# One encoder layer on one core: a second group of tile pairs by seven products in the last projection, with part of its weights prepared in the mixer

## The chip, the cores and the metric

The kernel runs on one core of one Trainium2 chip. The time is the device time of one execution, in microseconds (us), the median of several runs; one more execution was recorded by the hardware profiler, and every view below is of that one. Times inside a view count from the start of its span. The engines are TensorE (PE; PEld is its weight load), VectorE (DVE), ScalarE (ACT), GpSimd (POOL) and SyncE (SP, which here issues nearly all transfers).

## The reference

One layer of an encoder, on 512 tokens of width 1024, all in float32, with weights drawn at random:

```python
f = swiglu(rms_norm(h, ffn1_pre_g), ffn1_w1, ffn1_w3, ffn1_w2)   # (silu(x @ w1) * (x @ w3)) @ w2, D_FF = 2816
h = h + 0.5 * rms_norm(f, ffn1_post_g)
u = rms_norm(h, mix_pre_g)                                       # the mixer
q, k, v, xr, xg = split(u @ w_in)
y_a = (rg_lru(causal_conv(xr)) * gelu(xg)) @ w_lru_out
y_b = swa_sink_attention(q, k, v, sinks, bias) @ w_attn_out
g = sigmoid(u @ w_gate + b_gate)
h = h + rms_norm((g[0] * y_a + g[1] * y_b) @ w_o, mix_post_g)
f = swiglu(rms_norm(h, ffn2_pre_g), ffn2_w1, ffn2_w3, ffn2_w2)
h = h + 0.5 * rms_norm(f, ffn2_post_g)
```

The change is about the last matrix product of the second feed-forward part, `silu(...)*(...) @ ffn2_w2`: a hidden array of 2816 x 512 (features by tokens) against weights of 2816 x 1024, called w2b in the kernel. The first feed-forward part's is w2a.

## The kernel before

**Precision.** Each float32 operand is split into a high part (ScalarE copies it into the format that TensorE multiplies) and a low part (VectorE subtracts the high part from the operand). Each product is three matmuls: high by high, high by low, low by high.

**Stages.** w1a/w3a and w2a (first feed-forward part); the mixer, in the order xr, wg 0 to 7, wk, wv, wq, xg, then attention woven with lru, wq and wg 8 to 15, then wao and wo; w1b/w3b and w2b (second part). The 2816 features are 22 tiles of 128 rows. Most of w1/w3 is done by `Pairs`, which multiplies pairs of feature tiles by seven products of quarter blocks in place of eight (Winograd's form of Strassen's algorithm), on sums of blocks.

**w2_gemm.** The output (512 tokens by 1024) stands in all eight banks of PSUM as four token tiles by two halves. `W2[nm]` gives: how many tiles are multiplied plainly at first (24 matmuls of 512 columns a tile), how many pairs of tiles form the group that is multiplied by seven products, how many plain tiles come last (RF, four in w2b), and the planner's fill. In w2b it is 10 plain tiles, one group of 4 pairs, 4 last tiles. For a pair the hidden side is four quarters c (`h_plain`) and four sums of them s (`h_sums`), the weight side the blocks b11, b21 (`w_b1`), b22 and the sums t1, t2 (`w_t12`), t3 (`w_t34`) and t4 (`w_t4`), each with a high and a low part. `prod` runs one product over all pairs of the group (12 matmuls for each of two token tiles); between products banks are copied aside (`out_copy`, ScalarE, into tiles "kp") and added (`add_in`, VectorE). A group has a fixed cost of such copies and additions.

**Order of the work.** The program is laid out by hand. `point()` is called after every 12 matmuls or so; work is put on a list with `later(n, fn, rank)` and issued n points on. In `w2_gemm` a small planner gives each preparing step a due time (`PT` 5.44 a plain tile, `PB` 1.36 a product and pair) and a cost, goes through them backwards with `W2_LEAD` 2.5 us to spare and a fill of 0.95, and so finds the point at which each is issued. `task` issues a step's high part at once and its low part with the next step (`flush`).

**Memory.** All large tiles come from one pool of `NSLOT` = 43 slots of 4 KB a partition. An instruction whose result has no free slot waits until a slot's last reader is done. `uT` (32 KB a partition, outside the pool) holds the input of w1b/w3b and is lent to `w2_gemm` in eight regions of 4 KB. Transfers are issued by SP in program order (`dma_one`, `dma_to`), each also when its slot is free; a weight tile is 512 KB.

Of the kernel before, what the change touches and what calls it, by code (L numbers as in the profile page):

```python
# [51 lines left out]
def hybrid_layer(ctx: ExitStack, tc: tile.TileContext, a: dict, out: bass.AP):  # L52
# [42 lines left out]
    apart = {}  # L95

# [8 lines left out]
    def want_w2(name):  # L105

        first, n = W2[name][:2]
        apart.update((len(order) + first + i, i % 2) for i in range(2 * n))
        want(name, FT)
# [20 lines left out]

    loaded = set()
# [282 lines left out]

    def w2_gemm(nm, hid, gpost_name, scale, gpre_name, first, h_src, h_dst):

        W2_A, W2_S, RF, W2_FILL = W2[nm]
# [3 lines left out]
        pairs_ = list(range(W2_A, W2_A + 2 * W2_S, 2))  # L421

        def regions():
            for j in range(4):
                for e in range(2):
                    yield uT[:, e, 2 * j : 2 * j + 2, :].rearrange("p a b -> p (a b)")

        free_uT = list(regions())

        def room(name):  # L430
            return free_uT.pop(0) if free_uT else slot([P, D], F32R, name=name)

        def h_plain(f):
            H[f] = {"c": (room("ch"), room("cl"))}
            return H[f]["c"], hid.c[f].rearrange("p a b -> p (a b)")

        def h_sums(f):
            c = hid.c.pop(f)
            if any(x[0] is H[f]["c"][0] for x in pend):
                flush()  # L440
            a11, a12, a21, a22 = c[:, 0, :256], c[:, 1, :256], c[:, 0, 256:], c[:, 1, 256:]
            dve.tensor_tensor(out=a22, in0=a21, in1=a22, op=ALU.add)
            dve.tensor_tensor(out=a21, in0=a11, in1=a21, op=ALU.subtract)
            dve.tensor_tensor(out=a11, in0=a22, in1=a11, op=ALU.subtract)
            dve.tensor_tensor(out=a12, in0=a12, in1=a11, op=ALU.subtract)
            H[f]["s"] = (room("sh"), room("sl"))
            return H[f]["s"], c.rearrange("p a b -> p (a b)")

        def raw(f):
            if f not in W:  # L450
                k = base + f
                dma_to(k + 2)
                W[f] = {"r": (raws.pop(k), raws.pop(k + 1))}
            return W[f]["r"]

        def whole(f, a, b, src):
            hi, lo = slot([P, D], F32R, name="bh"), slot([P, D], F32R, name="bl")
            W[f][a] = (hi[:, :QH], lo[:, :QH])
            W[f][b] = (hi[:, QH:], lo[:, QH:])
            return (hi, lo), src  # L460

        def w_b1(f):
            return whole(f, "b11", "b21", raw(f)[0])

        def w_t12(f):
            r1, r2 = raw(f)
            s = slot([P, D], name="T12")
            dve.tensor_tensor(out=s[:, :QH], in0=r2[:, :QH], in1=r1[:, :QH], op=ALU.subtract)
            dve.tensor_tensor(out=s[:, QH:], in0=r2[:, QH:], in1=s[:, :QH], op=ALU.subtract)
            return whole(f, "t1", "t2", s)  # L470

        def w_t34(f):
            r1, r2 = raw(f)
            dve.tensor_tensor(out=r2[:, :QH], in0=r2[:, QH:], in1=r2[:, :QH], op=ALU.subtract)
            dve.tensor_tensor(out=r1[:, QH:], in0=r1[:, QH:], in1=r1[:, :QH], op=ALU.subtract)
            dve.tensor_tensor(out=r1[:, QH:], in0=r1[:, QH:], in1=r2[:, :QH], op=ALU.subtract)
            return whole(f, "t3", "b22", r2)

        def w_t4(f):
            r1 = W[f].pop("r")[0]  # L480
            t = slot([P, 2, QH], F32R, name="t4")
            W[f]["t4"] = (t[:, 0, :], t[:, 1, :])
            return W[f]["t4"], r1[:, QH:]

# [11 lines left out]
        def task(fn, f):  # L496
            one = fn(f)
            if one is not None:
                one = hi_part(*one)
            flush()  # L500
            if one is not None:
                pend.append(one)

        def tile_(k):
            dma_to(base + k + 1)
            hT = slot([P, 2, SEQ], F32R, name="hT")
            one = hi_part((hT[:, 0, :], hT[:, 1, :]), hid.f[k])
            hid.f[k] = None
            hid.t[k] = hT
            p = slot([P, D], F32R, name="whi"), slot([P, D], F32R, name="wlo")  # L510
            two = hi_part(p, raws.pop(base + k))
            pairs[base + k] = p
            st["split"] = base + k + 1
            flush()
            pend.extend((one, two))

        n0, F = W2_A + 2 * W2_S, FT - RF
        PT, PB = 5.44, 1.36 * W2_S
        ta = PT * W2_A
        tb = ta + 7 * PB  # L520
        tf = tb + PT * (F - n0)
        plan = [(PT * k, 1.75, tile_, k) for k in range(2, W2_A)]
        for i, f in enumerate(pairs_):
            d = 0.68 * i
            plan += [(ta + d, 1.14, h_plain, f), (ta + d, 1.14, w_b1, f), (ta + 2 * PB + d, 2.5, h_sums, f), (ta + 2 * PB + d, 2.4, w_t12, f)]
            plan += [(ta + 4 * PB + d, 3.0, w_t34, f), (ta + 6 * PB + d, 0.6, w_t4, f)]
        plan += [(tb + PT * (k - n0), 1.75, tile_, k) for k in range(n0, F)]
        plan += [(tf + 0.68 * (k - F), 1.75, tile_, k) for k in range(F, FT)]
        plan += [(ta + PB * (p + 0.5 * i + 0.5) + 1.5, 0.61, None, 0) for p in range(1, 7) for i in range(2)]
        plan.sort(key=lambda x: x[0])  # L530
        times = [PT / 2 * i for i in range(1, 2 * W2_A + 1)]
        times += [ta + PB / 2 * i for i in range(1, 15)]
        times += [tb + PT / 2 * i for i in range(1, 2 * (F - n0) + 1)]
# [17 lines left out]
        for k in range(2):  # L551
            w[k] = take(k)
        for tt in ((0, 1), (2, 3)):
            for t in tt:
                if t not in acc:
                    acc[t] = [bank("acc"), bank("acc")]
            for k in range(2):
                for t in tt:
                    mm_tok(acc[t], hid[k], t, w[k], k == 0, False)
                    if t % 2:  # L560
                        point()
# [11 lines left out]
        def add_in(b, name, i):  # L573
            dve.tensor_tensor(out=b, in0=b, in1=keep[name][:, i, :], op=ALU.add)

        for k in range(2, W2_A):
            w[k] = take(k)
            for t in range(NT):
                mm_tok(acc[t], hid[k], t, w[k], False, k == W2_A - 1)
                if k == W2_A - 1:  # L580
                    if t:
                        out_copy("z" if t < 2 else "y", t % 2, acc[t][1])
                    if t == 1:
                        out_copy("z", 0, acc[0][1])
                if t % 2:
                    point()
# [3 lines left out]
        st["get"] += 2 * W2_S  # L590
        def prod(b, i, ak, bk, start):
            for n_, f in enumerate(pairs_):
                wh, wl = W[f][bk]
                kind, blk = ak
                h, l = H[f][kind]
                c = slice(blk * 256 + i * P, blk * 256 + i * P + P)
                s_ = start and n_ == 0
                pe.matmul(b, h[:, c], wh, start=s_, stop=False, skip_group_check=True)  # L598
                pe.matmul(b, h[:, c], wl, start=False, stop=False, skip_group_check=True)  # L599
                pe.matmul(b, l[:, c], wh, start=False, stop=n_ == W2_S - 1, skip_group_check=True)  # L600

        def drop(*ks):
            for f in pairs_:
                for k_ in ks:
                    W[f].pop(k_)

        def fin(n, fn):
            later(n, fn, 0)

        for i in range(2):  # L610
            prod(Y[i], i, ("c", 0), "b11", True)
            out_copy("a", i, Y[i])
            point()
        for i in range(2):
            prod(X[i], i, ("c", 2), "b21", False)
            fin(1, lambda i=i: add_in(X[i], "a", i))
            point()
        for i in range(2):
            prod(Z[i], i, ("s", 3), "t1", True)
            dve.tensor_tensor(out=keep["y"][:, i, :], in0=Z[i], in1=keep["y"][:, i, :], op=ALU.add)  # L620
            point()
        drop("b11", "b21")
        for i in range(2):
            prod(Y[i], i, ("s", 0), "t2", False)
            dve.tensor_tensor(out=keep["z"][:, i, :], in0=Y[i], in1=keep["z"][:, i, :], op=ALU.add)
            point()
# [862 lines left out]
```

## Time and profile before

| | |
|---|---|
| median of 3 runs | 1131.6 us (1131.3 to 1131.66) |
| the profiled execution | 1131.66 us; its span 1129.9 us |
| granted TensorE clock | 0.998 of full |
| PE / DVE / ACT busy in the span | 1118.5 / 867.6 / 604.9 us |
| DMA | 131.23 MB, mean 116 GB/s |
| first matmul of w2b | 1007.60 us from the span's start |
| first and last matmul of its group | 1062.08 and 1100.11 us |

A line of a timeline has start, duration, engine, line of the kernel, operation, result<-operands, shapes, count, and in brackets the idle time of the engine before it and what ended that. Matmuls overlap, so one lasts 0.39 us while the next starts 0.23 us after it. "SPq" and "DVEq" are the queues of those engines.

### The profile page before, as it was taken

The numbers are of one execution on the slowest core, as the hardware profiler recorded it, in microseconds if no ns is written. First come the engines' busy times: TensorE is split into PE (matmuls) and PEld (weight loads), VectorE is DVE, ScalarE is ACT, GpSimd is POOL, SyncE is SP. The second block draws the span as 40 slices with busy tenths as digits, with TensorE's granted clock in tenths as the row PEclk, the third lists the DMA queues.
The fourth block names the chain that finished last, engine by engine and source line by source line (L and its number), as shares of the span: only waits on it lengthen the run. The fifth ranks groups of instructions, "written<-read, shape, count | busy, mean of one in ns | idle before, by whom it ended". The sixth has DMA issues, their size and how long they took to land.

```text
span 1129.9 us, 16956 instructions
## 1 busy us (share of the span) xinstructions
PE 1118.5 (99%) x6637; PEld 991.7 (88%) x6637; DVE 867.6 (77%) x1509; ACT 604.9 (54%) x1040; POOL 34.9 (3%) x60
## 2 busy tenths in 40 slices
PE   9999999999999999999999999999999999999997
PEld 7889999988888877888888888889899999998885
DVE  5999888889777746685889974667868888888595
ACT  7455554564555469844555663355545545574242
POOL 0000000000000000001111010000000000000000
PEclk9999999999999999999999999999999999999999
DMA  9872332250545212234222233342332332254033
GB/s 345 141 168 96 113 105 83 96 203 19 196 159 200 98 57 75 77 110 124 64 80 71 94 94 113 130 167 102 121 101 89 113 113 87 89 162 149 1 131 112
DMA packets 40577, 131.23 MB, mean 116 GB/s; under 512 B 4592, under 2 KB 6128, under 8 KB 40496
## 3 DMA queue, kind: packets, MB, share of 16 engines
q1 hardware_dynamic: 37904, 121.44, 31.9%
q0 software_dynamic: 2448, 8.43, 4.0%
q8 instruction: 52, 0.85, 0.3%
q10 hardware_dynamic: 144, 0.26, 0.1%
q14 instruction: 29, 0.24, 0.1%
HBM read 120.69 MB, written 9.43 MB: 115 GB/s over the span
## 4 chain that ended last, share of the span: by engine, by line
PE 88%; DVE 7%; ACT 4%; issue 1%; DMA 0%; SPq 0%; DVEq 0%; ACTq 0%
PE f L205 11%; PE f L207 11%; PE f L206 11%; PE c L711 10%; PE c L713 10%; PE c L712 10%; PE acc L223 4%; PE acc L224 4%; PE acc L225 4%; PE acc L598 2%; PE acc L600 2%; PE acc L599 2%; PE pt L1302 1%; ACT P L1279 1%; DVE P L1271 1%
## 5 line engine op out<-in xcount | busy, mean ns | idle before, releaser
L205 PE MATMUL f<-uT,whi 128*128 128x512 f32 (+1 forms) x536 | 197.1, 368 | 0.6 <-ACT uT L303 0.6
L207 PE MATMUL f<-uT,whi 128*128 128x512 f32 (+1 forms) x536 | 195.2, 364 | 0.4 <-DVE uT L304 0.4
L206 PE MATMUL f<-uT,wlo 128*128 128x512 f32 (+1 forms) x536 | 195.2, 364 | 0.0
L205 PEld LDWEIGHTS f<-uT,whi 128*128 128x128 f32 x536 | 101.1, 189 | 19.4 <-issue 2.9
L207 PEld LDWEIGHTS f<-uT,whi 128*128 128x128 f32 x536 | 101.1, 189 | 17.0 <-DVE uT L304 0.9
L711 PE MATMUL c<-Xh,whi 128*128 128x256 f32 x408 | 115.6, 283 | 0.1
L712 PE MATMUL c<-Xh,wlo 128*128 128x256 f32 x408 | 115.5, 283 | 0.0
L713 PE MATMUL c<-uT,whi 128*128 128x256 f32 x408 | 115.5, 283 | 0.0
L712 PE MATMUL c<-uT,wlo 128*128 128x256 f32 x408 | 115.5, 283 | 0.0
L713 PE MATMUL c<-Xl,whi 128*128 128x256 f32 x408 | 115.5, 283 | 0.0
L711 PE MATMUL c<-uT,whi 128*128 128x256 f32 x408 | 115.5, 283 | 0.0
L206 PEld LDWEIGHTS f<-uT,wlo 128*128 128x128 f32 x536 | 101.2, 189 | 15.3
L196 DVE TENSOR_TENSOR wlo<-S,whi 128x1024 fp32r<-128x1024 f32 x68 | 82.9, 1219 | 16.4 <-ACT whi L195 16.4
L223 PE MATMUL acc<-whi,hT 128*128 128x512 f32 x224 | 87.4, 390 | 0.0
L224 PE MATMUL acc<-wlo,hT 128*128 128x512 f32 x224 | 87.2, 389 | 0.0
L225 PE MATMUL acc<-whi,hT 128*128 128x512 f32 x224 | 87.1, 389 | 0.0
L711 PEld LDWEIGHTS c<-Xh,whi 128*128 128x128 f32 x408 | 78.3, 192 | 0.3 <-ACT ct L786 0.3
L712 PEld LDWEIGHTS c<-uT,wlo 128*128 128x128 f32 x408 | 78.3, 192 | 0.0
L711 PEld LDWEIGHTS c<-uT,whi 128*128 128x128 f32 x408 | 78.3, 192 | 0.0
L712 PEld LDWEIGHTS c<-Xh,wlo 128*128 128x128 f32 x408 | 78.3, 192 | 0.0
L713 PEld LDWEIGHTS c<-uT,whi 128*128 128x128 f32 x408 | 78.3, 192 | 0.0
L713 PEld LDWEIGHTS c<-Xl,whi 128*128 128x128 f32 x408 | 78.3, 192 | 0.0
(359 smaller groups left out, 2637.8 us busy)
## 6 DMA issues: line engine op xcount, KB each, us to landing
raw_w2a<-in_w2a_dram SPq DMA_DIRECT2D x22, 512.0 KB, 4.7
raw_w1b<-in_w1b_dram SPq DMA_DIRECT2D x22, 512.0 KB, 4.3
raw_w3b<-in_w3b_dram SPq DMA_DIRECT2D x22, 512.0 KB, 4.2
raw_w2b<-in_w2b_dram SPq DMA_DIRECT2D x22, 512.0 KB, 4.3
raw_w3a<-in_w3a_dram SPq DMA_DIRECT2D x21, 512.0 KB, 4.4
raw_w1a<-in_w1a_dram SPq DMA_DIRECT2D x20, 512.0 KB, 4.5
h<-h SPq DMA_DIRECT2D x16, 512.0 KB, 3.3
raw_wg<-in_wg_dram SPq DMA_DIRECT2D x16, 512.0 KB, 3.7
```

The source lines that it names most:

```text
L196: dve.tensor_tensor(out=lo, in0=src, in1=f32(hi), op=ALU.subtract)
L205: pe.matmul(ps[:, c0:c1], wh[:, s], h_, start=k == 0, stop=False)
L206: pe.matmul(ps[:, c0:c1], wl[:, s], h_, start=False, stop=False)
L207: pe.matmul(ps[:, c0:c1], wh[:, s], l_, start=False, stop=k == KT - 1)
L223: pe.matmul(acc[n], x[:, 0, c], wh[:, s], start=first, stop=False, skip_group_check=True)
L224: pe.matmul(acc[n], x[:, 0, c], wl[:, s], start=False, stop=False, skip_group_check=True)
L225: pe.matmul(acc[n], x[:, 1, c], wh[:, s], start=False, stop=last, skip_group_check=True)
L598: pe.matmul(b, h[:, c], wh, start=s_, stop=False, skip_group_check=True)
L599: pe.matmul(b, h[:, c], wl, start=False, stop=False, skip_group_check=True)
L711: pe.matmul(ps, wh[:, s], xh, start=first, stop=False, skip_group_check=True)
L712: pe.matmul(ps, wl[:, s], xh, start=False, stop=False, skip_group_check=True)
L713: pe.matmul(ps, wh[:, s], xl, start=False, stop=k == 3, skip_group_check=True)
```

## The change

`W2["w2b"]` goes from 10 plain tiles and one group of 4 pairs to 2 plain tiles and two groups of 4 pairs (tiles 2 to 9 and 10 to 17); the 4 last tiles stay. For five of the eight pairs (tiles 2, 4, 6, 8, 10: all of the first group, one of the second) the blocks b22 and the sums t1 to t4 are made earlier, in the mixer, split into high and low parts, written to DRAM, and loaded again in w2b; only b11/b21 are still made in w2b for them, and the second raw tile of such a pair is no longer loaded there. The steps of the hidden side and of the weights are cut finer, for w2a too: quarter c1 is no longer split (no product used it), the hidden sums come in two steps (`h_sums`, `h_rest`), and T3 and b22 are parts of their own. Tiles 2 and 3 of the hidden array are written directly into a shared slot (`hid.c`).

In the mixer, `pre_at(where)` stands in four places (ahead of xr, of xg, of each unit of the attention part, and of wao) and puts the steps of `pre_pair` on the list with the lowest rank:

```diff
+W2 = {"w2a": (6, (4,), 6, 0.95), "w2b": (2, (4, 4), 4, 0.95)}
+PRE = {"w2b": (2, 4, 6, 8, 10)}
+PRE_AT = {"xr": [("w2b", 2, 2, 2), ("w2b", 8, 21, 2)], "xg": [("w2b", 4, 1, 2)], ("wg", 13): [("w2b", 6, 1, 1)], "wao": [("w2b", 10, 4, 1)]}
+W2_LOAD = (14, 9, 8, 8)
...
+    def pre_pair(nm, f, at0, step):
...
+        dram = [tc.dram_tile([P, D], F32, name=f"pre_{nm}{f}_{i}") for i in range(5)]
...
+        def load():
+            for n in range(2):
+                r.append(slot([P, D], name="rawp"))
+                src = a[nm][f * P : (f + 2) * P, n * 512 : n * 512 + 512]
+                sp.dma_start(out=r[n].rearrange("p (b c) -> p b c", b=2), in_=src.rearrange("(b p) c -> p b c", p=P))
...
+        def store(i, name):
+            x = t.pop(name)
+            if i == 0:
+                for d, y in zip(dram[:2], x):
+                    sp.dma_start(out=d, in_=f32(y))
+            else:
+                sp.dma_start(out=dram[i + 1], in_=f32(x[2].rearrange("p a b -> p (a b)")))
...
+        steps = [
+            (load,),
+            (),
+            (lambda: hi("t12", t12_of(*r), D),),
+            (lambda: lo("t12"), lambda: hi("b22", r[1][:, QH:])),
+            (lambda: store(0, "t12"), lambda: lo("b22")),
+            (sums34, lambda: store(1, "b22")),
+            (lambda: lo("t3"), lambda: hi("t4", r[0][:, QH:])),
+            (lambda: store(2, "t3"), lambda: lo("t4"), lambda: r.clear()),
+            (lambda: store(3, "t4"),),
+        ]
+        for i, fns in enumerate(steps):
+            later(at0 + i * step, lambda fns=fns: [fn() for fn in fns], 4)
```

In `w2_gemm` (the planner, the loads and the loop over groups):

```diff
+        def h_plain(f):
+            if not h3:
+                t = slot([P, 4, 256], F32R, name="h3")
+                h3.extend((t[:, 2 * i, :], t[:, 2 * i + 1, :]) for i in range(2))
+            H[f, "c", 3] = h3.pop(0)
+            return [h_two(f, "c", 0, 2), (H[f, "c", 3], quarters(f)[:, 3, :])]
...
+        def w_load(f, i):
+            src = pre[f][i]
+            W.setdefault(f, {})
+            if i == 0:
+                (hi, lo), _ = whole(f, "t1", "t2", None)
+                sp.dma_start(out=f32(hi), in_=src[0])
+                sp.dma_start(out=f32(lo), in_=src[1])
+            else:
+                t = slot([P, 2, QH], F32R, name=("b22", "t3", "t4")[i - 1])
+                W[f][("b22", "t3", "t4")[i - 1]] = t[:, 0, :], t[:, 1, :]
+                sp.dma_start(out=f32(t.rearrange("p a b -> p (a b)")), in_=src)
...
+        for g in groups:
+            PB = 1.36 * len(g)
+            for i, f in enumerate(g):
+                d = 0.68 * i
+                plan += [(ta + d, 1.1, h_plain, f), (ta + d, 1.22, w_b1, f)]
+                plan += [(ta + 2 * PB + d, 2.1, h_sums, f), (ta + 4 * PB + d, 0.7, h_rest, f)]
+                if f in pre:
+                    loads += [(ta + p * PB + d, f, j) for j, p in enumerate((2, 4, 5, 6))]
+                else:
+                    plan += [(ta + 2 * PB + d, 2.6, w_t12, f), (ta + 4 * PB + d, 0.7, w_b22, f)]
+                    plan += [(ta + 5 * PB + d, 2.8, w_t3, f), (ta + 6 * PB + d, 0.7, w_t4, f)]
...
+        for due_, f, j in loads:
+            later(max(1, sum(x <= due_ - W2_LOAD[j] for x in times)), lambda f=f, j=j: w_load(f, j), 2)
...
+        for g in groups:
+            last = g is groups[-1]
...
+            def into(name, i, b, last=last):
+                add_in(b, name, i, None if last else keep[name][:, i, :])
```

`PRE_AT` entries are (matrix, first tile, first point, points between steps). `t12_of` and `t34_of` hold the sums that `w_t12` and `w_t34` had in place, in the same number of instructions; `whole` is unchanged. The `uT` regions of a group are lent again when its products no longer read them (`h_done`), and the additions of the first group go into the copies in SBUF where those of the last go into the banks (`into`).

More of the change, by code (lines that the diff above doesn't have):

```diff
@@ L105, in want_w2 @@
     def want_w2(name):
-        first, n = W2[name][:2]
-        apart.update((len(order) + first + i, i % 2) for i in range(2 * n))
+        first, ns = W2[name][:2]
+        apart.update((len(order) + first + i, i % 2) for i in range(2 * sum(ns)))
+        loaded.update(len(order) + f + 1 for f in PRE.get(name, ()))
         want(name, FT)
@@ L415, in w2_gemm, with pre_at @@
+    def pre_at(where):
+        for nm, f, at_, step in PRE_AT.get(where, ()):
+            pre_pair(nm, f, at_, step)
     def w2_gemm(nm, hid, gpost_name, scale, gpre_name, first, h_src, h_dst):
-        W2_A, W2_S, RF, W2_FILL = W2[nm]
+        W2_A, sizes, RF, W2_FILL = W2[nm]
+        n0, F = W2_A + 2 * sum(sizes), FT - RF
         base = order.index((nm, 0))
@@ L420, in w2_gemm @@
         w, H, W = {}, {}, {}
[L421 to L435, printed above, removed]
@@ L449, in raw @@
[L449 to L463, printed above, removed]
@@ L465, in w_t12 @@
[L465 to L483, printed above, removed]
+        groups, f = [], W2_A
+        for n in sizes:
+            groups.append(list(range(f, f + 2 * n, 2)))
+            f += 2 * n
         pend = []
@@ L496, in task, with room @@
         def task(fn, f):
-            one = fn(f)
-            if one is not None:
-                one = hi_part(*one)
+            new = [hi_part(*x) for x in fn(f)]
             flush()
-            if one is not None:
-                pend.append(one)
+            pend.extend(new)
+        spare = [uT[:, e, 2 * j : 2 * j + 2, :].rearrange("p a (b c) -> p (a b) c", b=2) for j in range(4) for e in range(2)]
+        lent, h3 = {}, []
+        def room(*key):
+            if spare:
+                lent[key] = spare.pop(0)
+                return lent[key]
+            return slot([P, 4, 256], F32R, name=f"h{key[0]}")
@@ new lines, in h_rest, with h_done, raw @@
+        def h_rest(f):
+            one = h_two(f, "s", 1, 2)
+            hid.c.pop(f)
+            return [one]
+        def h_done(*keys):
+            for f, kind, j in keys:
+                H.pop((f, kind, j))
+            for k in [k for k in lent if not any((k[1], k[0], j) in H for j in range(4))]:
+                spare.append(lent.pop(k))
+        def raw(f):
+            k = base + f
+            if "r" not in W.setdefault(f, {}):
+                dma_to(k + 2)
+                W[f]["r"] = raws.pop(k), raws.pop(k + 1, None)
+            return W[f]["r"]
@@ L515, in tile_ @@
-            pend.extend((one, two))
-        n0, F = W2_A + 2 * W2_S, FT - RF
-        PT, PB = 5.44, 1.36 * W2_S
+            return [((hT[:, 0, :], hT[:, 1, :]), c), (p, raws.pop(base + k))]
+        pre = PRE_TILES.get(nm, {})
+        PT = 5.44
         ta = PT * W2_A
-        tb = ta + 7 * PB
-        tf = tb + PT * (F - n0)
         plan = [(PT * k, 1.75, tile_, k) for k in range(2, W2_A)]
[L523 to L526, printed above, removed]
@@ L589, in w2_gemm @@
             w.pop(k)
[L590 to L605, printed above, removed]
+        st["get"] += 2 * sum(sizes)
         def fin(n, fn):
             later(n, fn, 0)
[L610 to L621, printed above, removed]
```

236 lines of the change are left out of this document (166 added, 70 removed).

## The prediction

> **What bounds the kernel now.** I read the page first (parts 1 and 4), then busy time by stage, then single instructions of the last stage.
>
> ```profile
> PE 1118.5 (99%) x6637; PEld 991.7 (88%) x6637; DVE 867.6 (77%) x1509; ACT 604.9 (54%) x1040; POOL 34.9 (3%) x60
> PE 88%; DVE 7%; ACT 4%; issue 1%; DMA 0%; SPq 0%; DVEq 0%; ACTq 0%
> ```
>
> TensorE is busy for 99% of the span and carries 88% of the chain. The columns of the next view are: stretch, its length, then busy us (and instructions) of PE, PEld, DVE, ACT, POOL, the clock, DMA share and GB/s. The first two rows are w2a up to the end of its group; the others are w2b.
>
> ```profile
> 232.00:267.30 35.30, 35.27 (x166) 29.29 (x164) 33.08 (x45) 18.77 (x22) 0.00 (x0) 1.00 0.33 114
> 267.30:305.50 38.20, 38.16 (x168) 31.62 (x169) 30.79 (x44) 15.71 (x22) 1.10 (x2) 1.00 0.34 111
> ...
> 1007.50:1018.40 10.90, 10.90 (x51) 9.04 (x50) 10.90 (x15) 7.73 (x10) 0.00 (x0) 1.00 0.44 143
> 1018.40:1029.30 10.90, 10.90 (x50) 9.03 (x49) 10.50 (x11) 6.03 (x6) 0.00 (x0) 1.00 0.93 343
> ...
> 1051.10:1062.20 11.10, 11.10 (x50) 8.96 (x50) 3.15 (x4) 2.52 (x4) 0.00 (x0) 1.00 0.00 0
> ```
>
> TensorE takes 50 or 51 matmuls in 10.9 to 11.1 us whether VectorE is full (10.90 of 10.90) or nearly idle (3.15 of 11.10): its own pace is the bound, and w2b before has VectorE to spare. In w2a VectorE ran at 94% (33.08 of 35.30) for 35 us and TensorE lost 0.03 us. So a full VectorE does not by itself stop the stage.
>
> The profiled execution took 1131.66 us (span 1129.9 and 1.76 around it), against a median of 1131.6; I sum against 1131.66.
>
> **The matmuls removed.** A plain pair of tiles takes 48 matmuls of 512 columns, a pair by seven products 42. These are the first matmul of w2b, the first of its group and the first after it:
>
> ```profile
> 1007.60 0.40 PE L223 MATMUL acc<-whi,hT 128*128 128x512 f32 x1
> ...
> 1062.08 0.50 PE L598 MATMUL acc<-bh,uT 128*128 128x512 f32 x1
> ...
> 1100.34 0.39 PE L223 MATMUL acc<-whi,hT 128*128 128x512 f32 x1
> ```
>
> Ten plain tiles: 54.48 us, 5.448 a tile. Four pairs by products: 38.26 us, 9.565 a pair, the restart at the group's head included. Four more pairs change over: 4 x (10.896 - 9.565) = **5.32 us off TensorE**, in a stretch where only its pace counts. [...]
>
> **VectorE in w2b.** Costs are steps from one start to the next:
>
> ```profile
> 1008.14 0.68 DVE L490 TENSOR_TENSOR hT<-sw,hT 128x512 fp32r<-128x512 f32 x1
> 1008.74 1.22 DVE L490 TENSOR_TENSOR wlo<-raw_w2b,whi 128x1024 fp32r<-128x1024 f32 x1
> 1009.88 0.69 DVE L490 TENSOR_TENSOR hT<-sw,hT 128x512 fp32r<-128x512 f32 x1
> ...
> 1031.86 0.42 DVE L442 TENSOR_TENSOR cc<-cc 128x256 f32<-128x256 f32 x1
> ...
> 1033.23 0.43 DVE L445 TENSOR_TENSOR cc<-cc 128x256 f32<-128x256 f32 x1
> 1033.57 0.69 DVE L468 TENSOR_TENSOR T<-raw_w2b,raw_w2b 128x512 f32<-128x512 f32 x1
> 1034.29 0.69 DVE L469 TENSOR_TENSOR T<-raw_w2b,T 128x512 f32<-128x512 f32 x1
> 1034.90 1.22 DVE L490 TENSOR_TENSOR sl<-cc,sh 128x1024 fp32r<-128x1024 f32 x1
> ...
> 1066.89 0.68 DVE L474 TENSOR_TENSOR raw_w2b<-raw_w2b 128x512 f32<-128x512 f32 x1
> ...
> 1068.82 1.22 DVE L490 TENSOR_TENSOR bl<-T,bh 128x1024 fp32r<-128x1024 f32 x1
> ```
>
> So 512 columns cost 0.60 us, 1024 cost 1.14, a tile (hT and w) 1.74, 256 columns 0.34; the four hidden sums 1.71 (1031.86 to 1033.57), the two sums of T12 1.33, the three of T34 1.93. After the change a pair's hidden side is 0.94 (c) + 1.71 + 0.60 + 0.60 = 3.85; its b11/b21 part 1.14; and, where the weights are not made earlier, 1.33 + 1.14 + 0.60 + 1.93 + 0.60 + 0.60 = 6.2. The stage then has 8 x 3.85 + 8 x 1.14 + 3 x 6.2 + 24 additions of banks x 0.60 + 4 last tiles x 1.74 = **80 us**. VectorE is free at 1008.1 and the last tiles are wanted from 1007.6 + 10.9 + 76.5 = 1095.0: 87 us, 92% full, less than in w2a. Measured by when things are wanted (from 1007.6): first group's c and b11 at 10.9, work to there 8.3; h_sums at 21.8, 9.2 more, so ready near 18.6; second group's sums at 60.0, 53.3 us of work so far; last tiles at 87.4, 78.8 us. With the 1.0 us in which VectorE starts late (0.5 for its last pair, 0.5 for uT, below) the margins are 1.6, 3.2, 5.7 and 7.6 us. The planner's rule with the new numbers asks its first task to start 0.8 us before the stage; for w2a before it asked 0.1 us.
>
> ScalarE makes the high parts ahead of it, faster (0.95 us for 1024 columns, 0.52 for 512, by the starts below); its first write to uT has to wait for the last matmul of the pairs, just before 1007.60, hence the 0.5 us.
>
> ```profile
> 1002.32 0.62 ACT L493 ACTIVATE hT<-sw 128x512 fp32r<-128x512 f32 x1
> 1002.84 1.05 ACT L493 ACTIVATE whi<-raw_w2b 128x1024 fp32r<-128x1024 f32 x1
> 1003.79 0.62 ACT L493 ACTIVATE hT<-sw 128x512 fp32r<-128x512 f32 x1
> ```
>
> **The loads.** Twenty-five of 0.52 MB (five a pair) come back from DRAM, on SP's queue ahead of the last tiles' weights and of the residual rows, and five raw tiles no longer come. The eight for T12 of the first group are 4.2 MB: 12.2 us at the 343 GB/s of the second row of w2b above, wanted at 21.8; with three raw tiles before them 16.8 us, and 2.8 more for landing (4.3 below, less 1.5 of transfer): 19.6. That is hidden by 2.2 us if slots are free.
>
> ```profile
> raw_w2b<-in_w2b_dram SPq DMA_DIRECT2D x22, 512.0 KB, 4.3
> ```
>
> **The slots** are my unknown. Counting what is alive when the fifth product of the first group runs (b22, t3, t4 12; the first group's s12 and c3 6; hidden tiles 6; kept banks 3; the second group's b11 8, raws 6, c 6) I get 47 against 43: four requests wait until product five ends (38.2), and those after until product six (43.6). The trace has such waits, in w2b before:
>
> ```profile
> 1040.24 0.69 DVE L468 TENSOR_TENSOR T<-raw_w2b,raw_w2b 128x512 f32<-128x512 f32 x1 [1.13 <-PE acc L224]
> ...
> 1045.75 1.22 DVE L490 TENSOR_TENSOR bl<-T,bh 128x1024 fp32r<-128x1024 f32 x1 [2.96 <-PE acc L224]
> ...
> 1019.57 1.06 ACT L493 ACTIVATE bh<-raw_w2b 128x1024 fp32r<-128x1024 f32 x1 [3.24 <-DMA raw_w2b<-in_w2b_dram]
> ```
>
> VectorE waits there for a plain tile's matmul to let a slot go, and ScalarE 3.24 us for a raw tile; there the parts were wanted 27 us later (1045.75 against 1062.08 + 10.9), so it cost nothing. Queued behind such a wait are all further parts and, on the same engines, the bank copies and additions that TensorE needs. I bound the standstill by 0 and by 5.4 + 3.2 = 8.6 us; the margin to the second group's sums is 5.7, so 0 to 2.9 reach TensorE. I take 0.8, nearer the rows of w2a, where 94% cost nothing.
>
> **The mixer.** Each of five pairs adds to VectorE 1.33 + 1.14 + 1.93 + 3 x 0.60 = 6.2 us, to ScalarE 0.95 + 3 x 0.52 = 2.5 us, and to SP two loads and five stores (3.7 MB, 10.7 us of transfer).
>
> ```profile
> 395.00:464.00 69.00, 69.00 (x323) 53.35 (x322) 39.17 (x55) 57.72 (x82) 0.00 (x0) 1.00 0.22 64
> 464.00:530.00 66.00, 66.00 (x330) 56.27 (x329) 46.68 (x56) 35.74 (x53) 5.46 (x12) 1.00 0.38 117
> 530.00:673.00 143.00, 142.22 (x740) 121.08 (x738) 120.03 (x357) 85.86 (x229) 18.48 (x26) 1.00 0.25 78
> 673.00:728.00 55.00, 55.00 (x248) 45.66 (x247) 28.52 (x36) 17.84 (x24) 2.13 (x2) 1.00 0.35 106
> ...
> 419.42 0.68 DVE L196 TENSOR_TENSOR xcs<-xc_t,xcs 128x512 fp32r<-128x512 f32 x1
> ...
> 426.47 0.49 PE L1106 MATMUL r<-xcs,rghi 64*128 64x512 f32 x1
> ```
>
> The pairs go where VectorE has room (two in xr to wq, one in xg, two behind wg 13 and in wao), and none into 530 to 673, the stretch with the only lost TensorE time. ScalarE is the tight one in the first row (84%), but the gates' operand is ready 6.4 us (420.1 to 426.5) before TensorE reads it, and one pair holds VectorE for at most 2 us at a time. A store makes SP wait for VectorE's part; behind it stand weights of units five places on. Bounds: 0 and 2 us of stalls; below nothing I see no reason. I take 0.4.
>
> **w2a** gets the finer steps too: per pair 0.1 us less VectorE work (3.85 for 3.99, 3.13 for 3.07), and 3 us of it moves from ahead of its group to behind. TensorE lost 0.03 us there: nothing to gain, cover kept. Tiles 2 and 3 written straight to their place cost nothing, on the same instruction.
>
> **Sum:** 1131.66 - 5.32 + 0.8 + 0.4 = **1127.5 us**.
>
> **Rivals.**
> - *VectorE late, gain mostly lost.* The standstill reaches its 8.6 us and the mixer its 2: 1131.66 - 5.32 + 2.9 + 2.0 = 1131.2, no change to measure. For: 92% full, slots short. Against: w2a's rows. Another road to no change is that TensorE's pace is not the bound: nothing is gained, 1131.7. Against it stand the equal counts of matmuls above. [...]
> - *Loads chained to slots: slower.* If the four loads of a product (b22, t3, t4 of the first group) only get slots when the product before the last lets its own go, they take 4 x 1.5 + 2.8 = 8.9 us with one product of 5.47 to hide it: 3.4 us of stall for each. From two such products on the gain is gone; with all three it is 1131.66 - 5.32 + 10.3 + 0.4 = 1137.0. For: 47 against 43, and loads asked only 8 to 9 us ahead. Against: T12's eight slots come free a product earlier. [...]
> - *The mixer stands: slower.* The sums sit in VectorE's queue and wait for their two loads; SP's own waits for slots there reach 10.1 us:
>
> ```profile
> SPq L142 <- PE pt L1302: 10.1, 1, 10.1
> ...
> raw_wao<-in_wao_dram SPq DMA_DIRECT2D x8, 512.0 KB, 3.6
> ```
>
> With 3.6 of landing and 5.5 between request and sums, the step of two pairs, VectorE stands 8 us; units are split two ahead (10.9 us), so it shows only if two such waits meet: about 8 us, 1134.7.
>
> **Chances.** My forecast (1126.2 to 1129.3) 0.55; no change 0.17; chained loads 0.18; the mixer 0.10. A measurement of this kernel can tell about 0.2% (2.3 us) from no change: faster 0.55, same 0.17, slower 0.28. The forecast's own range is 1126.0 to 1129.3; for 8 in 10 it must reach through "no change" and into the chained loads up to their price: 1125.9 to 1137.0.
>
> **What would show it.** Right: w2b's seven-product part about 76.5 us long with 336 matmuls, its start near 1007.6 plus the mixer's loss, VectorE over 85% busy through it, no gap above 0.3 us on TensorE but at heads of groups. Wrong: TensorE waiting for a DMA of pre_w2b or for a lo part on VectorE in products 3 to 7 of the first group; a w2b start later than 1008.5; or the last tiles' matmuls waiting for VectorE.

## The result and the profile after

Slightly slower: 1133.69 us in the median of 20 runs (1131.86 to 1135.11) against 1131.63 for the kernel before (20 runs, 1131.11 to 1131.95). The ratio is 1.0020, with a 95% interval of 1.0013 to 1.0027. I had forecast 1127.5, 4.1 us faster than before; it is 2.1 us slower. The time lies inside my range, 1125.9 to 1137.0, on the side to which I gave 0.28.

The profiled execution took 1135.11 us, the longest of the 20; its span is 1133.3. These lines of its page answer to those of before: busy time, the chain, and the group of matmuls that read low parts of feature weights (matmul | busy us, mean ns | idle us before them, releaser).

```profile
PE 1117.4 (99%) x6613; PEld 989.7 (87%) x6613; DVE 904.0 (80%) x1601; ACT 617.7 (55%) x1088; POOL 35.0 (3%) x60
PE 80%; DVE 11%; ACT 6%; issue 3%; DVEq 0%; ACTq 0%
L206 PE MATMUL f<-uT,wlo 128*128 128x512 f32 (+1 forms) x536 | 195.4, 365 | 2.3 <-DVE wlo L161 2.3
```

The 24 matmuls are gone (6637 to 6613), VectorE and ScalarE hold 17% of the chain where it was 11%, and TensorE now waits for low parts. First the busy times in w2b by stretch (columns as in the prediction): its two plain tiles, its first and its second group.

```profile
1016.05:1026.95 10.90, 10.90 (x51) 8.94 (x50) 10.34 (x19) 8.54 (x15) 0.00 (x0) 1.00 0.85 337
1026.95:1065.20 38.25, 38.25 (x171) 31.68 (x170) 30.25 (x55) 16.67 (x27) 0.00 (x0) 1.00 0.72 266
1065.20:1103.50 38.30, 37.74 (x166) 30.78 (x165) 36.51 (x58) 18.30 (x29) 0.53 (x1) 1.00 0.41 146
```

And its first matmul, the first after the groups, and TensorE's only wait there (waits of TensorE from 1008 us on: us in total, times, longest):

```profile
1016.16 0.40 PE L223 MATMUL acc<-whi,hT 128*128 128x512 f32 x1
...
1104.18 0.39 PE L223 MATMUL acc<-whi,hT 128*128 128x512 f32 x1
```

```profile
PE acc L714 <- DVE bl L499: 0.6, 1, 0.6
```

So w2b did what was forecast: 88.02 us to the last tiles for 92.74 before (1007.60 to 1100.34), 4.72 less, the 5.32 of the matmuls and one wait of 0.6. But it begins at 1016.16 in place of 1007.60: 8.56 us are lost ahead of it. I subtracted the start of each matmul before from that of the same matmul after. The difference stays near zero up to 484 us, is 2.78 at 498, 5.51 at 567, 8.44 at 574, and hardly moves from there to w2b. TensorE in these places, after:

```profile
485.82 0.50 PE L206 MATMUL f<-uT,wlo 128*128 128x512 f32 x1 [1.16 <-DVE wlo L161]
498.19 0.50 PE L206 MATMUL f<-uT,wlo 128*128 128x512 f32 x1 [1.15 <-DVE wlo L161]
...
567.50 0.44 PE L1395 MATMUL s<-KS,QS 128*128 128x128 f32 x1 [2.43 <-DVE QS L1344]
...
570.49 0.63 PE L205 MATMUL f<-y,whi 128*128 128x512 f32 x1
570.92 0.63 PE L206 MATMUL f<-y,wlo 128*128 128x512 f32 x1
```

Three parts, then: two stops for xg's low parts (2.78 with what follows each), a stop for QS, the queries, in attention (2.73), and behind it matmuls at 0.43 us apart in place of 0.23, until 573.9 (2.93). In the last part nothing is waited for; the granted clock there is 0.50 (the columns are those of the stretches of w2b), and 1.00 from 574 to 580:

```profile
567.50:573.90 6.40, 6.34 (x16) 5.03 (x17) 6.22 (x18) 2.67 (x10) 0.73 (x1) 0.50 0.27 84
```

### The profile page after: what moved, and what is told of

Same layout as the page of the kernel before. It is cut to its first block, busy times and chain, and to the rows that moved or that the text cites. A ratio compares the mean times of both kernels' runs of the same rounds, so it can differ in the third digit from the quotient of the medians.

```text
span 1133.3 us, 17197 instructions
## 1 busy us (share of the span) xinstructions
PE 1117.4 (99%) x6613; PEld 989.7 (87%) x6613; DVE 904.0 (80%) x1601; ACT 617.7 (55%) x1088; POOL 35.0 (3%) x60
## 4 chain that ended last, share of the span: by engine, by line
PE 80%; DVE 11%; ACT 6%; issue 3%; DVEq 0%; ACTq 0%
PE c L839 10%; PE c L841 10%; PE c L840 10%; PE f L205 9%; PE f L207 8%; PE f L206 8%; PE acc L223 4%; PE acc L225 4%; PE acc L224 4%; PE acc L714 3%; PE acc L715 3%; PE acc L713 3%; DVE wlo L161 2%; ACT P L1409 1%; DVE P L1401 1%
## 5 line engine op out<-in xcount | busy, mean ns | idle before, releaser
L195 ACT ACTIVATE whi<-S 128x1024 fp32r<-128x1024 f32 x68 | 68.2, 1050 | 0.0
L223 PE MATMUL acc<-whi,hT 128*128 128x512 f32 x160 | 62.5, 390 | 0.0
L224 PE MATMUL acc<-wlo,hT 128*128 128x512 f32 x160 | 62.3, 389 | 0.0
```

Of the source, the lines that this page charges most:

```text
L195: act.activation(hi, src, AF.Copy)
L223: pe.matmul(acc[n], x[:, 0, c], wh[:, s], start=first, stop=False, skip_group_check=True)
L224: pe.matmul(acc[n], x[:, 0, c], wl[:, s], start=False, stop=False, skip_group_check=True)
```

## Experiments

All times are medians; each ratio is to runs of the kernel before on the same chip, with its 95% interval. The diffs on placement show only the part of `PRE_AT` that changes. For the first nine kernels my theory, called V, was that VectorE's added work in two places delays what TensorE reads; the rival D was the transfers. Theory V fell halfway, as the third group of runs shows.

### Which part of the change, and what in it

The mixer's part alone (w2b as before, the prepared tiles unused):

```diff
-W2 = {..., "w2b": (2, (4, 4), 4, 0.95)}
-PRE = {"w2b": (2, 4, 6, 8, 10)}
+W2 = {..., "w2b": (10, (4,), 4, 0.95)}
+PRE = {}
```

> The five pairs are made, split and stored in the mixer as in the change, but w2b is multiplied as before (10 plain tiles, one group of 4) and doesn't read them. If the mixer costs 8.4 us in the profiled run and the second group gains 5 us (the shifts between the traces): 1136.5 to 1140, 5.5 to 8.4 above before, all of the loss before wo. If instead part of the loss comes from w2b's second group or from its loads: 1131.6 to 1134.

Measured: 1138.49 us, ratio 1.0061 (1.0048 to 1.0073), 6.95 above before. The loss is the mixer's.

The whole change without the engines' work for the pairs in the mixer; the transfers stay:

```diff
-            (lambda: hi("t12", t12_of(*r), D),),
-            (lambda: lo("t12"), lambda: hi("b22", r[1][:, QH:])),
-            (lambda: store(0, "t12"), lambda: lo("b22")),
...
+            (),
+            (),
+            (lambda: store(0),),
```

> The change without VectorE's and ScalarE's work for the five pairs in the mixer: the two raw tiles are loaded and stored as they are, five stores at the same points, so w2b multiplies unsplit weights. Theory V (VectorE's added work delays xg's low parts and attention): the mixer is back to before's times, w2b gains 5 us, 1126.6. Theory D (transfers, SP's queue and slots delay the mixer): as the change, 1133 to 1134. Between them, 1129 to 1131, if both count.

Measured: 1127.08 us, 0.9961 (0.9949 to 0.9974), 4.5 us below before. D is out as the main cause: seven transfers a pair, with SP's waits for slots, cost 0.8 us, in two waits for QS at 562, and most of w2b's gain is left. (Here no store has to wait for VectorE's part. In the change SP does wait so, but neither VectorE nor ScalarE waits for a transfer between 380 and 574 us there.)

The finer steps alone:

```diff
+W2 = {"w2a": (6, (4,), 6, 0.95), "w2b": (10, (4,), 4, 0.95)}
+PRE = {}
+PRE_AT = {}
```

> None of the pairs is made in the mixer and w2b has one group as before; only the finer steps of the hidden side and the weights remain, in w2a and w2b, and the hidden tiles written straight to their place. My prediction gave them nothing: 1131.6, within 0.1% of before. If the finer steps carry a part of the gain: 1130 or less.

Measured: 1130.98 us, 0.9996 (0.9987 to 1.0005): no difference that could be told, as predicted.

### Which pair, and where

```diff
-"xr": [("w2b", 2, 2, 2), ("w2b", 8, 21, 2)]
+"xr": [("w2b", 2, 2, 2), ("w2b", 8, 3, 2)]
```

> Tile 8's pair alone is moved from points 21 to 37 (wq and xg) to points 3 to 19, beside tile 2's pair. Theory V: the 2.8 us that TensorE loses on xg's low parts by 500 us are gone; tile 4's pair still delays VectorE by some 2 us at the start of attention, so 0 to 2.7 us of the wait for QS stay, with or without the 2.9 us at a lower clock behind it: 1126.6 to 1132. Theory D: the transfers are as many and as near: 1133 to 1134.

Measured: 1129.68 us, 0.9979 (0.9970 to 0.9987). The stops at xg are gone; waits for QS of 1.9 us in all and a stretch of matmuls 0.43 us apart remain (rows in the last section). Moving tile 4's pair instead:

```diff
-"xg": [("w2b", 4, 1, 2)], ("wg", 13): [("w2b", 6, 1, 1)]
+("wg", 13): [("w2b", 6, 1, 1), ("w2b", 4, 2, 2)]
```

> Tile 4's pair alone is moved from xg to the stretch behind wg 13, beside tile 6's and tile 10's pairs. Theory V: the 2.8 us on xg's low parts stay; VectorE enters attention only as late as TensorE does, so the wait for QS is under 1 us and the clock stays: 1126.6 + 2.8 to 3.6 = 1129.4 to 1130.2. If the wait for QS comes from tile 8's pair as well: 1132 to 1134. If VectorE is too full behind wg 13 (59 of 62 us of work by then) a new wait shows before wo.

Measured: 1132.15 us, 1.0005 (0.9996 to 1.0014). The stops at xg stay (2.5 us), TensorE waits 0.4 us for QS, as before the change, and matmuls stay 0.23 us apart behind it (mean granted clock 0.998, for 0.996 in the change); but the new place was too full, with 3.2 us lost around wo, as TensorE's waits from 670 to 760 us show:

```profile
PE acc L223 <- DVE g L1508: 1.1, 1, 1.1
PE f L206 <- DVE wlo L161: 0.6, 1, 0.6
PE acc L224 <- DVE wlo L161: 0.3, 1, 0.3
```

So it takes tile 8's pair for the stops at xg, and tile 4's for that at QS; tile 8's makes the latter longer (2.4 us with both, 1.1 and 0.3 with tile 4's alone). Tile 8's pair in fewer points:

```diff
-("w2b", 8, 21, 2)
+("w2b", 8, 21, 1)
```

> Tile 8's pair in its place of the change but with its nine steps at every point in place of every second: points 21 to 29, some 452 to 474 us, before the stretch in which VectorE was 94% busy without it (480 to 500). Theory V (the stretch decides): the wait for xg's low parts falls from 2.8 to under 1 us, the rest is as with tile 8 moved further ahead, 1129.5 to 1131.5. If it is the amount of VectorE work ahead of the scans, wherever it stands: 1133 to 1134.

Measured: 1134.15 us, 1.0021 (1.0012 to 1.0030), a miss: TensorE now stops 1.4 us in wv and 1.4 at xg, and still waits for QS. That the stretch from 480 to 500 alone decides was wrong; 452 to 474, where ScalarE was busy for 19.3 of 22 us before, is no better.

### VectorE, ScalarE, or the links between them

ScalarE's copies alone, then VectorE's sums and low parts alone, in their places:

```diff
 # ScalarE alone                           # VectorE alone
+(lambda: hi(r[0], D),),                   +(lambda: t.update(T=t12_of(*r)),),
+(lambda: hi(r[1][:, QH:]),),              +(lambda: t.update(l=lo(t.pop("T"), D)),),
+(lambda: store(0),),                      +(lambda: store(0, t.pop("l")), lambda: lo(r[1][:, QH:])),
...
```

> The kernel with transfers alone, with ScalarE's four copies a pair put back in their places (of raw tiles, their result not used; VectorE's work for the pairs is left out, w2b multiplies unsplit weights). If VectorE's share alone makes the loss: 1127.1 to 1127.6, as the transfers alone. If ScalarE's copies make a part of it: 1128.5 or more, with TensorE waiting for xg's low parts or QS.

> The same with VectorE's sums and low parts in their places (a tile less itself in place of a tile less its high part) and no copies of ScalarE; w2b multiplies unsplit weights. If VectorE's share alone makes the loss: 1133 to 1134, with the stops at 484, 495 and 562 of the change. If it takes ScalarE's copies and the waits on them as well: 1130 or less.

Measured: 1127.28 us, 0.9963 (0.9949 to 0.9976), and 1126.37 us, 0.9956 (0.9943 to 0.9968). Neither alone costs clearly more than the transfers did, so VectorE's amount of work by itself, my theory V, isn't the cause. The traces name a link between the engines. ScalarE in the change, and in the kernel that has VectorE's work alone:

```profile
452.27 0.82 ACT L1251 ACTIVATE xc_t<-xc_t,chalf 128x512 f32<-128x512 f32 x1
454.89 1.06 ACT L447 ACTIVATE ph<-T 128x1024 fp32r<-128x1024 f32 x1 [1.80 <-DVE T L418]
455.85 0.67 ACT L1238 ACTIVATE xc_t<-r,bhalf 64x512 f32<-64x512 f32 x1
...
466.39 1.99 ACT L160 ACTIVATE whi<-raw_wq 128x1024 fp32r<-128x1024 f32 x2
```

```profile
453.26 0.69 ACT L1225 ACTIVATE xc_t<-r,bhalf 64x512 f32<-64x512 f32 x1 [0.55 <-PE r L1221]
...
463.29 1.99 ACT L160 ACTIVATE whi<-raw_wq 128x1024 fp32r<-128x1024 f32 x2
```

`hi("t12", t12_of(*r), D)` puts a sum on VectorE and, in the same step, a copy of that sum on ScalarE. The copy stands at the head of ScalarE's queue until VectorE reaches the sum, and the gates' work for the scans stands behind it (it begins at 455.85, though the last of TensorE's matmuls for it, 0.39 us long, began at 453.21): 1.80 us of waiting and 1.0 of copying less the 0.55 that ScalarE had to spare here. It is 2.6 us late at the gates (455.85 for 453.26; 0.4 of it from earlier) and, with one more copy, 3.1 us late at wq. VectorE gets its scans that much later and, with tile 8's work among them, cannot make it up (rows below). The same again for tile 4's pair, ScalarE and then VectorE in the change:

```profile
509.53 1.06 ACT L447 ACTIVATE ph<-T 128x1024 fp32r<-128x1024 f32 x1 [2.15 <-DVE T L418]
510.49 1.04 ACT L160 ACTIVATE whi<-raw_xg 128x1024 fp32r<-128x1024 f32 x1
```

```profile
511.57 1.23 DVE L161 TENSOR_TENSOR wlo<-raw_xg,whi 128x1024 fp32r<-128x1024 f32 x1 [2.13 <-ACT whi L160]
```

The wait comes back to VectorE: it made ScalarE late by 2.15 us and then stands 2.13 itself, for the high part that was queued behind the copy. ScalarE waits as long for tile 8's T34, but VectorE has no idle time behind that wait, so it isn't passed on:

```profile
481.23 0.63 ACT L447 ACTIVATE pb<-rawp 128x512 fp32r<-128x512 f32 x1 [2.81 <-DVE rawp L422]
```

First test of the link: the sums one step ahead of their copies, at all five places.

```diff
-            (lambda: hi("t12", t12_of(*r), D),),
+            (lambda: t.update(T=t12_of(*r)),),
+            (lambda: hi("t12", t.pop("T"), D),),
...
-            (sums34, lambda: store(1, "b22")),
+            (lambda: t34_of(*r), lambda: store(1, "b22")),
+            (lambda: hi("t3", r[1][:, :QH]),),
```

> The change with all five pairs at its own places, but T12 and T34 are each issued one step (two points in xr and xg) ahead of the high parts made of them; the work on both engines is the same. Theory H (the loss comes from ScalarE standing in order behind a sum that is still to come on VectorE, 1.8 us at 453 and 2.8 us at 478 us of the change, which neither engine's work shows alone): ScalarE's chain is late by its two copies only, 1.6 us less than in the change by 465, and TensorE's stops at 484 to 495 fall from 2.8 to under 1 us, those at QS from 2.7 to under 1.5: 1126.7 to 1129.7. Rival (both engines' work together is too much for these places, in whatever order): 1132 or more, with the stops of the change.

Measured: 1131.94 us, 0.9998 (0.9989 to 1.0007), half a hit: the loss at xg falls from 2.78 to 0.78 us, but QS still costs 2.8 and the low clock behind it 2.8 (mean granted clock 0.996). ScalarE still waits 4.2 us for T34, and the two added steps push tile 8's last parts among xg's outputs (499 and 503 us), so it does not separate link from work.

Second test: all the work of both engines, without links.

```diff
-            (lambda: hi("t12", t12_of(*r), D),),
-            (lambda: lo("t12"), lambda: hi("b22", r[1][:, QH:])),
+            (lambda: hi(r[0], D), lambda: t.update(T=t12_of(*r))),
+            (lambda: t.update(l=lo(t.pop("T"), D)), lambda: hi(r[1][:, QH:])),
...
```

> VectorE's sums and low parts and ScalarE's four copies a pair all in the change's places, the same number and sizes, but neither reads what the other made (copies of raw blocks, a tile less itself as the low part); w2b multiplies unsplit weights. Theory H (the links between the engines make the loss): 1126.4 to 1128. Theory W (the sum of both engines' work is too much here: VectorE, without slack, is driven by ScalarE, which is late by its own copies, 1.6 us): stops of 0.8 us or more at xg and 1 us or more at QS, 1129 to 1132.

Measured: 1127.12 us, 0.9962 (0.9948 to 0.9975). One stop of 0.78 us at xg is left, TensorE waits 0.4 us for QS as before, and matmuls stay 0.23 us apart behind it (mean granted clock 0.998). So the 6.6 us between this kernel and the change in the medians go with the links. (Here parts also give their slots back sooner, since nothing reads them. In the change every wait of 1 us or more of VectorE and ScalarE from 450 to 535 us ends with an operand that they read, none with a slot, so this is no rival.)

VectorE's first low part for xg that TensorE stops for, in the change, both unlinked, and the kernel with tile 8's pair moved:

```profile
484.57 1.20 DVE L161 TENSOR_TENSOR wlo<-raw_xg,whi 128x1024 fp32r<-128x1024 f32 x1
```

```profile
482.09 1.20 DVE L161 TENSOR_TENSOR wlo<-raw_xg,whi 128x1024 fp32r<-128x1024 f32 x1
```

```profile
483.18 1.20 DVE L161 TENSOR_TENSOR wlo<-raw_xg,whi 128x1024 fp32r<-128x1024 f32 x1
```

In the change VectorE does the same work as unlinked, with no idle time from 476.1 to 503 us, and stays 2.48 us behind throughout: this is the delay from 453. With tile 8's pair moved ScalarE is as late at wq (466.93 us), by links of the same kind, and VectorE begins its scans even later (477.69 for 477.15); but tile 8's sums are not among them, the low part is 1.4 us earlier than in the change, and TensorE loses nothing at xg. So it takes both: a link that makes VectorE late, and added work behind it that fills VectorE until TensorE reads.

When VectorE comes to attention's first scores, in before, the change, VectorE alone, and both unlinked:

```profile
531.24 0.35 DVE L1271 CUSTOM_DVE_ANT_0 P<-s,BT,vec 128x128 f32<-128x128 f32 x1 [0.45 <-PE s L1266]
```

```profile
536.01 0.35 DVE L1401 CUSTOM_DVE_ANT_0 P<-s,BT,vec 128x128 f32<-128x128 f32 x1
```

```profile
531.07 0.35 DVE L1388 CUSTOM_DVE_ANT_0 P<-s,BT,vec 128x128 f32<-128x128 f32 x1 [0.51 <-PE s L1383]
```

```profile
531.69 0.35 DVE L1391 CUSTOM_DVE_ANT_0 P<-s,BT,vec 128x128 f32<-128x128 f32 x1 [0.45 <-PE s L1386]
```

In three of them VectorE waits for TensorE there; in the change it comes 4.8 us late, 2 more than TensorE itself by then, and QS, made on VectorE, inherits that: by the QS that TensorE stops for it is 5.8 us late (566.68 for 560.87 before, rows further below). Less the 2.8 us by which TensorE itself is late, and some 0.3 that QS had to spare before, this is the stop of 2.7.

### The clock behind a stop

The change with nine matmuls into a bank that is overwritten next, where TensorE stands for QS:

```diff
             ps = bank("s")
+            if (g, j, hp) == (1, 0, 1):
+                for _ in range(9):
+                    pe.matmul(ps, uT[:, 0, 0, :P], uT[:, 0, 0, :], start=True, stop=True)
```

> The change with nine matmuls of 512 columns into a bank that is overwritten next, ahead of the scores that wait 2.4 us for QS (2.04 us at 0.227 us each). Theory C (the wait itself costs its length, and the half clock behind it 2.9 us more, because TensorE stood): the wait shrinks to 0.4 us, the pitch of 0.43 us behind it is gone, 1130.8 in the median of the change, with less spread than its 1131.9 to 1135.1. Rival (the clock falls for another reason than standing still, such as the kind of work): the same time as the change, 1133.7, with the pitch of 0.43 us still there.

Measured: 1131.92 us (1131.62 to 1132.46), 1.0004 (0.9996 to 1.0013); 1.8 us below the change in the median, 3.1 between the two profiled executions. TensorE in its trace:

```profile
564.52 2.27 PE L1393 MATMUL s<-uT 128*128 128x512 f32 x9
567.04 0.33 PE L1398 MATMUL s<-KS,QS 128*128 128x128 f32 x1 [0.25 <-DVE QS L1344]
...
569.08 0.39 PE L205 MATMUL f<-y,whi 128*128 128x512 f32 x1
569.31 0.39 PE L206 MATMUL f<-y,wlo 128*128 128x512 f32 x1
```

QS is no earlier, but behind it the matmuls are 0.23 us apart again, for 0.43 in the change, and the mean granted clock of the execution is 0.999, for 0.996: the low clock came from standing still. The spread agrees: the change's 20 runs go from 1131.86 at a mean clock of 0.998 to 1135.11 at 0.996, while all 11 runs here have 0.998 or 0.999.

### A better version

Tile 8's pair beside tile 2's, tile 4's in the seven-product part of w1b/w3b:

```diff
+    pre_at("w1b")
     pairs_b.run(w2_ahead)
...
-"xr": [("w2b", 2, 2, 2), ("w2b", 8, 21, 2)], "xg": [("w2b", 4, 1, 2)]
+"xr": [("w2b", 2, 2, 2), ("w2b", 8, 3, 2)], "w1b": [("w2b", 4, 2, 6)]
```

> Tile 8's pair beside tile 2's (points 3 to 19), and tile 4's pair spread over the seven-product part of w1b/w3b, one step every 6 points. Theory V: neither xg nor attention nor wo loses anything; only the mixer's 0.3 us beside tile 2's pair and the 0.5 us of the kernel with transfers alone remain: 1126.6 to 1127.6, below before by 0.35 to 0.45%. If VectorE has no room in w1b/w3b either (83% busy before): gaps of 0.5 to 2 us on TensorE at products there, 1128 to 1131. If w2b's loads or slots were the trouble: no better than moving tile 8's pair alone, 1129.7.

Measured: 1131.63 us, 1.0001 (0.9992 to 1.0010). Nothing is lost in the mixer, but there is one stop in w1b, by the same link, before it was known as such (ScalarE, then TensorE):

```profile
851.02 1.06 ACT L447 ACTIVATE ph<-T 128x1024 fp32r<-128x1024 f32 x1 [7.59 <-DVE T L418]
851.98 0.37 ACT L914 ACTIVATE ct<-c 128x256 f32<-128x256 f32 x1
```

```profile
852.40 0.58 PE L839 MATMUL c<-Xh,whi 128*128 128x256 f32 x1 [3.17 <-ACT ct L914]
```

The copy of a bank (`ct`) that frees it for TensorE stood behind the copy of a sum that VectorE had not begun: it starts at 851.98, though TensorE had begun its last matmul ahead of the stop at 848.95. The stop cost 3.2 us and the low clock behind it 2.7 (mean granted clock 0.996, for 0.998 in the next kernel). Then the same placement, with tile 4's sums a step (six points) ahead of their copies, by the diff of the first test of the link, applied to that pair alone:

> As the kernel with both pairs moved, but for tile 4's pair, in w1b/w3b, the sums T12 and T34 are a step of their own, six points ahead of the high parts made of them, so that ScalarE isn't held by a copy whose sum is still queued on VectorE. Theory V with that cause of the 3.2 us stop and the 2.7 us at half clock behind it: both are gone, 1131.6 - 5.9 = 1125.5 to 1127, the best of all kernels. If VectorE's room in w1b/w3b is the cause, not the order on ScalarE: a stop of 1 us or more stays, 1128 to 1132.

Measured: 1126.65 us (1126.31 to 1126.93), 0.9956 (0.9942 to 0.9969), faster than before and than the change. Against the last kernel only the link is taken out, which puts tile 4's later steps six to twelve points back; that is worth 5.0 us. Of TensorE's waits from the mixer on, only those that stand in before and the one in w2b are left:

```profile
PE acc L728 <- DVE bl L513: 0.6, 1, 0.6
PE s L1409 <- DVE QS L1358: 0.4, 1, 0.4
...
PE s L1409 <- ACT es L1424: 0.3, 1, 0.3
...
```

The links of tiles 2, 6, 8 and 10 are still in this kernel, and ScalarE waits up to 3.8 us for their sums, but TensorE stops for none of it: a link need not cost TensorE anything.

## Why the prediction was wrong

**The matmuls removed: right.** 5.32 us, by rows; w2b's three stretches above show it, and the best version reaches 1126.65 because of it. The pace before, 227 ns a matmul (5.448 us for the 24 of a plain tile), holds: the 48 of the two plain tiles took 10.90 us (1016.16 to 1027.06).

**VectorE and loads in w2b: right, a little too dear.** I took 0.8 us and got 0.6, in one wait of the second group, at 1079 us, for the low part of a T12 (`bl<-T`) made there. VectorE did 77.1 us of work in 87.45, where I had 80 in 87. The two groups took 337 matmuls in 76.55 us, for 336 in 76.5. The chained loads, my strongest rival with 0.18, did not come: no wait of TensorE in products 3 to 7 of the first group, so whatever the slots delayed, TensorE did not see it.

**The mixer: the step that failed.** I wrote 0.4 us, between 0 and 2; it was 8.56 in the profiled execution, the slowest of the 20, and 6.95 in the medians of the mixer alone. The sign that I had put down for it, a start of w2b later than 1008.5, came at 1016.16. Three things in that paragraph were wrong. "The pairs go where VectorE has room" was read from busy shares. VectorE's work fits there but for one stop of 0.78 us, as the kernel without links shows, so the room was real, but it did not answer the question. That the gates' operand "is ready 6.4 us (420.1 to 426.5) before TensorE reads it" took one cover, at 426 us, for the whole stretch; at 453 us, ahead of ScalarE's part of the same gates, its spare time is 0.55 us. And "one pair holds VectorE for at most 2 us at a time" counted the engine that works, not the one that waits for it: I listed the waits of SP for the stores but not ScalarE's wait for the sum that was issued in the same step, although the diff has it in one expression. What was queued behind that wait (the gates and with them the scans, high parts of xg) made late what TensorE read next.

**The rival on the mixer** had nearly the number, 1134.7, and the wrong mechanism: VectorE waiting for late loads. VectorE has no wait for these loads from 380 us to w2b. Its price of 8 us was worked out from a wait of SP and a landing time, with no row of ScalarE in it, so that it comes near the 8.56 is luck. (Its sum leaves out the 0.8 of w2b; with it, it gives 1135.1.) It is luck, too, that the time lies in my range: the range went up so far for the chained loads, which did not come.

**No price for the clock.** 2.93 of the 8.56 us are matmuls at a granted clock of 0.50 behind a stop. I had priced every stop at its length.

**A sign that I passed over.** In before, VectorE finishes the second half of the QS that the change stops for at 562.27 us, and TensorE reads that half at 562.42. VectorE before, TensorE before, and VectorE after:

```profile
560.87 1.40 DVE L1215 SCALAR_TENSOR_TENSOR QS<-f,QS 64x512 fp32r<-64x512 f32 x2
```

```profile
562.42 0.30 PE L1265 MATMUL s<-KS,QS 128*128 128x128 f32 x1
```

```profile
566.68 1.40 DVE L1344 SCALAR_TENSOR_TENSOR QS<-f,QS 64x512 fp32r<-64x512 f32 x2
```

Among TensorE's waits in the mixer of before stands one of the same kind, for a later QS, at 631 us:

```profile
PE s L1265 <- DVE QS L1215: 0.4, 1, 0.4
```

So this chain had almost no spare time at either place, and my sum had no part for it.

## What to carry to other kernels

When work is added to two engines in a chain, ask for each instruction what it waits for when it gets to the head of its queue, and what of the old work stands behind it (here 1.80 us of waiting for one sum, and its copy, put ScalarE's work for the gates 2.2 us back); busy shares of either engine do not tell that. Issue a producer on one engine ahead of its consumer on the other, in a place where the chain to TensorE has spare time, and look for that time at each reader, not at one. One step ahead was enough in w1b/w3b, where it is six points; at the places of the change, where it is one or two, ScalarE still waited 4.2 us. When a sum has parts in several stages, run each stage alone: here the mixer alone (7.0 us slower than before) and the change with only its transfers in the mixer (4.5 us faster) showed in two runs what lay under a result of 2 us.

## What the runs showed of the hardware

A short stop cost more than its length here: TensorE ran at a granted clock of 0.50, 0.43 us a matmul, for about 6 us behind a stop of 2.43 us. In the kernel with tile 8's pair moved, stops of 1.13 and 0.32 us, with short matmuls between, came ahead of such a stretch too; 1.4 us after the second, matmuls were 0.43 us apart for 3.4 us, each 0.61 to 0.63 us long, as at the clock of 0.50 in the change:

```profile
563.62 0.30 PE L1395 MATMUL s<-KS,QS 128*128 128x128 f32 x1 [1.13 <-DVE QS L1344]
564.34 0.30 PE L1395 MATMUL s<-KS,QS 128*128 128x128 f32 x1 [0.32 <-DVE QS L1344]
...
565.78 0.61 PE L206 MATMUL f<-y,wlo 128*128 128x512 f32 x1
566.19 0.63 PE L207 MATMUL f<-y,whi 128*128 128x512 f32 x1
...
569.43 0.39 PE L206 MATMUL f<-y,wlo 128*128 128x512 f32 x1
```

In the profile of the denser tile 8 a stop of 2.4 us had no such stretch behind it (mean clock 0.998); nor had the two stops of 1.2 us at xg in the change (1.00 from 480 to 505 us), nor the stop of 0.4 us for QS in before (1.00 from 628 to 640 us) or that in the best version (mean clock 0.998). With tile 8's pair moved, 1.45 us of stops in two pieces cost 1.6 us more: 3.40 us for eight matmuls, where the pace of 227 ns gives 1.82. What the short matmuls between the two stops did was not tried, and why one stop had such a stretch behind it and another of the same length had none was not shown.
